# A convolution block split between ScalarE and GpSimd, in a one-core decoder-layer kernel on Trainium2

## The chip, the cores and the metric

The kernel runs on one core of one Trainium2 chip. A core has a matrix engine (TensorE, PE in the profile), three engines that work on whole tiles (VectorE or DVE, ScalarE or ACT, GpSimd or POOL), a queue engine for transfers (SyncE or SP), an on-chip memory of 128 partitions (SBUF) and an accumulator memory (PSUM). Each engine runs its own instructions in the order in which they were written into the program, and waits on semaphores for the others.

The metric is the device time of one execution in microseconds (us). The median of three runs before the change is 1310.73 us.

## The reference

One layer of a decoder over 1,024 tokens of 1,024 channels: RMS norm, one input projection, a token mixer whose two halves work side by side (an RWKV-7 head group of 8 heads and a causal convolution of 512 channels and 31 taps), an output projection, and a gated feed-forward network with a short convolution of its own. The part that the change touches is the convolution:

```python
c = u[..., :D_CONV] * jax.nn.sigmoid(u[..., D_CONV:])
c = _causal_dwconv(c, cconv_w, cconv_b)        # 31 taps, each channel by itself
c = jax.nn.silu(_layer_norm(c, cln_g, cln_b))  # over the 512 channels
mix = jnp.concatenate([rwkv_out, c], axis=-1) @ w_out
```

Each channel's output is a sum over 31 shifted copies of its input, each times one weight, plus a bias. All is in float32.

## The kernel before, in words

The tokens are worked in two halves of 512 (`h` 0 and 1), each of two quarters (0 to 3). Channels lie on partitions, tokens run along the tile. Matrix products are made exact by splitting both operands into a high and a low part: a weight tile `wr` comes by DMA, ACT casts it to `wh`, and POOL (or a kept copy in memory) supplies the low part `wl` (L158); every product is then three matmuls (`h` by `wh`, the low part of `h` by `wh`, `h` by `wl`). The names `h_314`, `h_315` and so on are these pairs for one block of normed channels, written by ACT (L271, high) and DVE (L273, low).

The convolution has four blocks of 128 channels for each half, `conv(h, i)`. Its input `c` (128 x 542, with the 30 tokens before the half) is made by `glu_in`. `conv` keeps a running sum `acc` in the PSUM bank `pc`, of which there is one. ACT starts it with the first tap and the bias (L407), DVE adds the other thirty taps, one instruction for each (L410), and the last of them writes the result `co` to SBUF. `conv_norm` then transposes the four `co` of a half on PE and normalises them, and `w_out` projects them.

The mixer's recurrence is worked by quarter. A quarter's `inverses` inverts small triangular blocks with a chain of 28 short instructions on DVE, alternately L585 (`sub`, a product) and L587 (`dw`, a sum), with all tensors in SBUF. In front of it stand two transposes (L576), and POOL sets parts of `dw` with memsets (L578, L579). `merge` takes the chain's result: a transpose (L595), two more (L599), and PE's matmuls `pe<-dw,l` in between. Then chunks of 64 tokens run in sequence through `recurrence`, with PE writing `xs`, DVE adding state (`r`, L719), and POOL or ACT scaling states (`XG`, L700, L698). PE's projection of the second half is interleaved with this.

The order of the work is set by a scheduler: each part is written in a stream that has a priority number, and the scheduler places instructions on each engine by priority and by its own estimate of times, so that a change in one block moves others.

```python
PRIO = {"first": -1000, "top": 100000, "rwkv": 1000, "norm": 200000, "conv": 300000, "proj": 400000}
BUFS = {..., "co": 4, "po": 1, "c": 4, "t2": 2}
```

The smaller number comes first. In addition `conv(0, 2, W[1].mark)` and `conv(0, 3, W[1].mark)` are held until the last transpose (L599) of quarter 1's `merge` has been issued. The tag `t2` (two buffers of 128 x 512 in SBUF) is used for the normalised rows in `conv_norm` and for one copy in `glu_in`.

Of the kernel before, what the change touches and what calls it, by code (L numbers as in the profile page):

```python
# [15 lines left out]
AF = mybir.ActivationFunctionType  # L16
ALU = mybir.AluOpType
# [4 lines left out]
P = 128  # L22
# [3 lines left out]
HALF = 512  # L26
# [9 lines left out]
CONV_W = 31  # L36
# [58 lines left out]
class Trunk:  # L95
# [281 lines left out]
    def glu_in(self, h, hs, st, i):  # L377
# [19 lines left out]
            nc.gpsimd.tensor_copy(self.ccarry[:, i], c[:, HALF:])  # L397
        st["c", i] = c


    def conv(self, st, i):

        nc = self.nc
        c, co, acc = st["c", i], self.tl("co", [P, HALF]), self.bank("pc")
        st["co", i] = co
        w = lambda j: self.par("cw", i * CONV_W + j)
        nc.scalar.activation(acc, c[:, :HALF], AF.Identity, scale=w(0), bias=self.par("cb", i))  # L407
        for j in range(1, CONV_W):
            out = co if j == CONV_W - 1 else acc
            nc.vector.scalar_tensor_tensor(out, c[:, j:j + HALF], w(j), acc, ALU.mult, ALU.add)  # L410
# [671 lines left out]
    def mixer(self, sts):  # L1082
        nc, tc = self.nc, self.tc
        W = [None] * 4
        mixes = [None] * 2

        def project(h, hs, names):
            with self.stream("proj"):
                for n in names.split():
                    if n == "w":  # L1090
                        self.wa_in(h, hs, sts[h])
                    elif n == "g":
                        self.gate_in(h, hs, sts[h])
                    elif n[0] == "u":
                        self.glu_in(h, hs, sts[h], int(n[1]))
                    else:
                        self.rkv_in(h, hs, sts[h], (n[0], int(n[1])))

        def weave(*parts):

            with self.stream("rwkv"):
                parts = list(parts)
                while parts:
                    parts = [p for p in parts if next(p, parts) is None]

        def quarter(q):
            W[q] = SimpleNamespace(off=(q % 2) * QUARTER, st=sts[q // 2], GD=[], bon=[], R=[], CA=[], CK=[])
            return self.elementwise(W[q])
# [43 lines left out]
        def conv(h, i, behind=None):  # L1152

            with ExitStack() as gate, self.stream("conv"):
                if behind is not None:
                    gate.enter_context(tc.issue_after(behind.ins))
                self.conv(sts[h], i)

        def conv_norm(h):
            with self.stream("conv"):  # L1160
                self.conv_norm(sts[h])
# [28 lines left out]
        prepare(0)  # L1190
        project(0, hs, "u0 u1")
        conv(0, 0)
        conv(0, 1, W[0].mark)
        project(0, hs, "u2 u3")
        hs = self.pairs("h")
# [2 lines left out]
        prepare(1)  # L1198
        project(1, hs, "k0 k1 w r0 r1")
        weave(quarter(2))  # L1200
        conv(0, 2, W[1].mark)
        conv(0, 3, W[1].mark)
        conv_norm(0)
        project(1, hs, "u0 u1 u2 u3")
        prepare(2)
# [104 lines left out]
```

## Time and profile before

| | before |
|---|---|
| median of 3 runs | 1310.73 us (1307.76 to 1311.3) |
| profiled execution, time | 1310.48 us |
| its span in the profile | 1308.7 us |
| mean granted clock of TensorE | 0.984 |
| PE busy | 1260.4 us |
| DVE busy | 864.0 us |
| ACT busy | 678.4 us |
| POOL busy | 462.6 us |

The span runs from the first to the last instruction; the time of the execution is 1.8 us longer. Busy time of an engine is no bound by itself: what counts in a stage is which engine the others wait for there. A row of a group reads: line, engine, operation, result and operands with their shapes, count, busy time and mean length of one in ns, then the engine's idle time in front of them and who ended it. A row of the timeline reads: start, length, engine, line, operation, operands, count, and in square brackets the idle time in front with its releaser. In a table by stage each engine's busy time stands with the number of its instructions.

In the profiled execution `conv(0, 2)` runs on DVE from 243 to 271 us and `conv(0, 3)` from 273 to 306 us; its input `c` is there at 188 us.

### The profile page before, as it was taken

How to read it: one execution, taken by the hardware profiler on the slowest of the kernel's cores; microseconds unless marked ns; L12 is line 12 of the kernel's file. 1: busy time of each engine (PE TensorE's matmuls, PEld its weight loads, DVE VectorE, ACT ScalarE, POOL GpSimd, SP SyncE). 2: the span in 40 equal slices, each digit the busy share in tenths (PEclk: the TensorE clock that was granted, in tenths of full speed). 3: DMA queues.
4: the chain of work that ended last, by engine and by line, in shares of the span. 5: the costliest groups of instructions: out<-in, count | busy, mean ns of one | idle time of the engine just before them, and what ended most of it. 6: DMA issues, size and time to landing. Idle time of an engine off the chain costs nothing.

```text
span 1308.7 us, 22940 instructions
## 1 busy us (share of the span) xinstructions
PE 1260.4 (96%) x8580; PEld 1018.6 (78%) x8580; DVE 864.0 (66%) x1520; ACT 678.4 (52%) x1354; POOL 462.6 (35%) x412
## 2 busy tenths in 40 slices
PE   5999989999999989999999999999999999999996
PEld 4767767777779867878799788888888888888884
DVE  5276997996789989995521364355455438479567
ACT  6563663656855765657642464443433445444451
POOL 4343320111123322444462466676766540000001
PEclk9999989999999989999999999999999999999998
DMA  6554332243333351222354765666564433335326
GB/s 236 160 146 125 115 112 90 83 145 113 115 110 106 119 181 43 73 66 78 100 161 126 265 211 167 194 183 195 173 207 137 120 92 113 94 110 164 105 65 209
DMA packets 97167, 176.77 MB, mean 135 GB/s; under 512 B 10560, under 2 KB 17088, under 8 KB 97056
## 3 DMA queue, kind: packets, MB, share of 16 engines
q1 hardware_dynamic: 97056, 175.31, 43.5%
q8 instruction: 67, 1.10, 0.4%
q14 instruction: 44, 0.36, 0.1%
HBM read 139.62 MB, written 35.65 MB: 134 GB/s over the span
## 4 chain that ended last, share of the span: by engine, by line
PE 77%; DVE 14%; ACT 4%; DMA 2%; issue 2%; POOL 1%; SPq 0%; POOLq 0%; ACTq 0%; DVEq 0%
PE pb L131 63%; PE pe L131 5%; DVE pc L410 4%; PE pn L131 3%; PE xs L131 3%; DVE dw L587 1%; PE pe L146 1%; DMA x<-x1d 1%; DVE pt L479 1%; DVE nrow L971 1%; DMA pt<-mixd 1%; DVE kk L480 1%; POOL wl L158 1%; PE pc L146 0%; DVE m L158 0%
## 5 line engine op out<-in xcount | busy, mean ns | idle before, releaser
L131 PE MATMUL pb<-f,wh 128*128 128x512 f32 x1408 | 444.5, 396 | 3.6 <-ACT pb L782 1.8
L158 POOL TENSOR_TENSOR wl<-wr,wh 128x512 fp32r<-128x512 f32 (+1 forms) x240 | 316.3, 1319 | 360.9 <-ACT wh L158 332.4
L158 ACT CAST wh<-wr 128x512 fp32r<-128x512 f32 (+1 forms) x279 | 171.5, 615 | 296.0 <-PE pb L131 142.3
L131 PEld LDWEIGHTS pb<-f,wh 128*128 128x128 f32 x1408 | 265.1, 189 | 63.9 <-ACT pb L782 2.0
L131 PE MATMUL pb<-f,wl 128*128 128x512 f32 x704 | 280.6, 399 | 1.7 <-POOL wl L158 1.5
L131 PE MATMUL pb<-h,wh 128*128 128x512 f32 (+3 forms) x720 | 230.0, 399 | 1.9 <-ACT wh L158 1.0
L888 DVE SCALAR_TENSOR_TENSOR acc<-pb,params,acc 128x511 f32<-128x511 f32 (+1 forms) x128 | 95.4, 745 | 184.8 <-ACT acc L883 124.0
L410 DVE SCALAR_TENSOR_TENSOR pc<-c,params,pc 128x512 f32<-128x512 f32 x232 | 174.1, 751 | 8.3 <-ACT pc L407 4.4
L131 PEld LDWEIGHTS pb<-f,wl 128*128 128x128 f32 x704 | 133.1, 189 | 34.6 <-POOL wl L158 3.9
L131 PEld LDWEIGHTS pb<-h,wh 128*128 128x128 f32 (+2 forms) x720 | 132.0, 189 | 34.4 <-ACT wh L158 2.7
L131 PE MATMUL pb<-h,wl 128*128 128x512 f32 (+3 forms) x360 | 146.3, 406 | 2.7 <-POOL wl L158 2.5
L153 POOL TENSOR_TENSOR ss<-var,mhalf 128x1 f32<-128x1 f32 x16 | 11.0, 693 | 229.7 <-DVE ss L952 203.3
L131 PE MATMUL pb<-w,a 128*128 128x512 f32 x366 | 89.8, 393 | 0.0
L131 PEld LDWEIGHTS pb<-h,wl 128*128 128x128 f32 (+2 forms) x360 | 67.8, 188 | 21.8 <-POOL wl L158 5.1
L131 PE MATMUL pb<-wh,a 128*128 128x512 f32 x240 | 81.5, 396 | 0.0
L131 PEld LDWEIGHTS pb<-w,a 128*128 128x128 f32 x366 | 68.7, 188 | 16.1
L928 POOL TENSOR_TENSOR b<-b,b 128x512 f32<-128x512 f32 x44 | 57.0, 1295 | 0.9
L888 DVE SCALAR_TENSOR_TENSOR pt<-pb,params,pt 128x511 f32<-128x511 f32 (+1 forms) x48 | 35.7, 744 | 31.5 <-ACT ecarry L885 31.0
L131 PEld LDWEIGHTS pb<-wh,a 128*128 128x128 f32 x240 | 45.1, 188 | 10.6
L700 POOL TENSOR_TENSOR XG<-r,GE 64x256 f32<-64x256 f32 x30 | 20.8, 696 | 85.5 <-DVE r L719 80.8
L883 ACT ACTIVATE acc<-pb,params 128x512 f32<-128x512 f32 x64 | 49.5, 773 | 1.8 <-PE pb L131 1.8
L131 PE MATMUL pb<-wl,a 128*128 128x512 f32 x120 | 47.7, 397 | 0.0
(301 smaller groups left out, 2038.8 us busy)
## 6 DMA issues: line engine op xcount, KB each, us to landing
wr<-ffn_up SPq DMA_DIRECT2D x176, 256.0 KB, 2.7
wr<-w_in SPq DMA_DIRECT2D x80, 256.0 KB, 2.9
b<-ffn_down SPq DMA_DIRECT2D x44, 256.0 KB, 3.9
sums<-b SPq DMA_DIRECT2D x44, 256.0 KB, 2.4
wr<-sums SPq DMA_DIRECT2D x44, 256.0 KB, 2.7
lows<-wl SPq DMA_DIRECT2D x40, 256.0 KB, 3.2
wl<-lows SPq DMA_DIRECT2D x40, 256.0 KB, 2.6
wr<-ffn_down SPq DMA_DIRECT2D x33, 256.0 KB, 2.7
```

The costliest lines, as they stand in the source:

```text
L131: return self.nc.tensor.matmul(out, lhsT, rhs, start=start, stop=stop, skip_group_check=skip)
L146: self.nc.tensor.transpose(out, in_, self.con("ident")[:n, :n])
L158: return self.nc.scalar.copy(hi, src), eng.tensor_tensor(lo, src, hi.bitcast(F32), ALU.subtract)
L410: nc.vector.scalar_tensor_tensor(out, c[:, j:j + HALF], w(j), acc, ALU.mult, ALU.add)
L479: nc.vector.tensor_tensor_scan(sg[:, l], self.con("scan"), sg[:, l], 0.0, ALU.mult, ALU.add)
L480: nc.vector.scalar_tensor_tensor(kk[:, l], k[:, l], self.par("k_k", 2 * pp + l), kk[:, l], ALU.mult, ALU.mult)
L587: nc.vector.tensor_tensor(dv[:, j + 1:, :j], dv[:, j + 1:, :j], tv, ALU.add)
L700: nc.gpsimd.tensor_tensor(x[64:128], R[64:128, gs], w.GE[64:128, c, gs].unsqueeze(2).broadcast_to([64, 4, CH]), ALU.mult)
L883: nc.scalar.activation(acc, ps, AF.Identity, scale=w(2), bias=self.par("fb", ch))
L888: nc.vector.scalar_tensor_tensor(acc[:, o:], ps[:, :HALF - o], w(j), acc[:, o:], ALU.mult, ALU.add)
L928: sub = lambda o, x, y, op=ALU.subtract: nc.gpsimd.tensor_tensor(o, x, y, op)
L971: nc.vector.tensor_tensor(out, a, b, op)
```

## The change

One block, `conv(0, 3)`, is computed by a new function. ACT writes the first tap with the bias into `co` in SBUF, then multiplies each of the other thirty taps into a tile `ct` (tag `t2`), and POOL adds each tile to `co`. PSUM and DVE have no part in it. The call stands ahead of that for `conv(0, 2)` and is not held by `W[1].mark`. `conv(0, 2)` and all other blocks stay as they were.

```diff
+    def conv_pool(self, st, i):
+
+        nc = self.nc
+        c, co = st["c", i], self.tl("co", [P, HALF])
+        st["co", i] = co
+        w = lambda j: self.par("cw", i * CONV_W + j)
+        nc.scalar.activation(co, c[:, :HALF], AF.Identity, scale=w(0), bias=self.par("cb", i))
+        for j in range(1, CONV_W):
+            ct = self.tl("t2", [P, HALF])
+            nc.scalar.activation(ct, c[:, j:j + HALF], AF.Copy, scale=w(j))
+            nc.gpsimd.tensor_tensor(co, co, ct, ALU.add)
...
-                self.conv(sts[h], i)
+                (self.conv_pool if (h, i) == (0, 3) else self.conv)(sts[h], i)
...
+        conv(0, 3)
         conv(0, 2, W[1].mark)
-        conv(0, 3, W[1].mark)
         conv_norm(0)
```

The new lines shift those below them by 12: what is L578 in the kernel before is L590 after. Its own lines are L407 (first tap), L410 (taps) and L411 (adds).

The scheduler places the new instructions among those of other streams, at three places that matter here. The first is ACT where the second half's channels are handed to PE. `c_305` is the block's input, `h_314` and `h_316` the first two channel pairs. Before:

```order
L698 COPY XG_356_2135<-xs0_95 64x256
L698 COPY XG_357_2138<-xs1_96 64x256
L641 COPY l8_207_1125<-pe_247_1486 32x8x32
L271 ACTIVATE h_314_1928<-pe_330_1944,params_72 128x512
L271 ACTIVATE h_316_1930<-pb_331_1951,params_72 128x512
```

After:

```order
L710 COPY XG_356_2135<-xs0_95 64x256
L710 COPY XG_357_2138<-xs1_96 64x256
L653 COPY l8_207_1125<-pe_247_1486 32x8x32
L410 ACTIVATE t2_492_3150<-c_305_1882,params_72 128x512
L410 ACTIVATE t2_493_3153<-c_305_1882,params_72 128x512
L271 ACTIVATE h_314_1928<-pe_330_1944,params_72 128x512
L271 ACTIVATE h_316_1930<-pb_331_1951,params_72 128x512
```

Two taps now stand ahead of the first copy of the channels; on DVE, four L410 of `conv(0, 1)` (L422 after) stand ahead of the first L273, where two stood.

The second place is POOL around quarter 1's inverse chain, from the memsets of `dw` at its start to the memset of `l8_366` behind its end (L604 before, L616 after). `co_491` is the block's sum, `t2_...` the taps, `wl_439` and `wl_442` are low parts of weights. Before:

```order
L158 TENSOR_TENSOR wl_439_2857<-wr_437_2854,wh_438_2856 128x256
L578 MEMSET dw_98 128x16x16
L579 MEMSET dw_98 128x16
L158 TENSOR_TENSOR wl_442_2875<-wr_440_2872,wh_441_2874 128x256
L700 TENSOR_TENSOR XG_394_2592<-r_383_2272,GE_130_729 64x256
L604 MEMSET l8_366_2208 32x32x32
```

After:

```order
L590 MEMSET dw_98 128x16x16
L411 TENSOR_TENSOR co_491_3148<-co_491_3148,t2_507_3195 128x512
L591 MEMSET dw_98 128x16
L411 TENSOR_TENSOR co_491_3148<-co_491_3148,t2_508_3198 128x512
L411 TENSOR_TENSOR co_491_3148<-co_491_3148,t2_509_3201 128x512
L158 TENSOR_TENSOR wl_439_2857<-wr_437_2854,wh_438_2856 128x256
L411 TENSOR_TENSOR co_491_3148<-co_491_3148,t2_510_3204 128x512
L712 TENSOR_TENSOR XG_394_2592<-r_383_2272,GE_130_729 64x256
L411 TENSOR_TENSOR co_491_3148<-co_491_3148,t2_511_3207 128x512
L411 TENSOR_TENSOR co_491_3148<-co_491_3148,t2_512_3210 128x512
L158 TENSOR_TENSOR wl_442_2875<-wr_440_2872,wh_441_2874 128x256
L616 MEMSET l8_366_2208 32x32x32
```

Six adds now stand between the memsets, fifteen stand before them and nine behind.

The third place is PE where it takes the chain's result (`pe_386<-dw_98`). `pb_436` and `pb_444` are projection sums. Before:

```order
L131 MATMUL pb_436_2853<-h_328_1942,wl_442_2875 64x512
L146 MATMUL xs1_96<-const_73,v_163_906 64x128 x2
L131 MATMUL pb_444_2895<-h_314_1928,wh_446_2898 128x512
L131 MATMUL pb_444_2895<-h_315_1929,wh_446_2898 128x512
L131 MATMUL pe_386_2329<-dw_98,l8_342_2059 32x16 x64
```

After:

```order
L131 MATMUL pb_436_2853<-h_320_1934,wl_439_2857 64x512
L131 MATMUL pb_436_2853<-h_322_1936,wh_441_2874 64x512
L131 MATMUL pb_436_2853<-h_323_1937,wh_441_2874 64x512
L131 MATMUL pe_386_2329<-dw_98,l8_342_2059 32x16 x64
L131 MATMUL xs0_95<-r_383_2272,l8_186_1034 64x64
```

Before, all 24 matmuls of `pb_436` and two of `pb_444` stand ahead of it; after, 14 of `pb_436`. The other ten and the two of `pb_444` follow.

On DVE the L410 of `conv(0, 3)` are gone; the first statistics of half 0's normalisation follow two instructions behind the last tap of `conv(0, 2)`.

## The prediction

> **What bounds the kernel now.** I read the page's busy times first, then a table of busy time by stage, then the two lines that carry the convolution, and only then single instructions around it.
>
> ```profile
> PE 1260.4 (96%) x8580; PEld 1018.6 (78%) x8580; DVE 864.0 (66%) x1520; ACT 678.4 (52%) x1354; POOL 462.6 (35%) x412
> PE 77%; DVE 14%; ACT 4%; DMA 2%; issue 2%; POOL 1%; SPq 0%; POOLq 0%; ACTq 0%; DVEq 0%
> L410 DVE SCALAR_TENSOR_TENSOR pc<-c,params,pc 128x512 f32<-128x512 f32 x232 | 174.1, 751 | 8.3 <-ACT pc L407 4.4
> ```
>
> TensorE (PE) is busy 96% of the span and carries 77% of the chain that ended last; VectorE (DVE) carries 14%. The convolution's multiply-adds (L410) are the largest DVE group, 751 ns each. By stage (columns: stretch and its length, then PE, PEld, DVE, ACT, POOL busy, PE clock, DMA share, GB/s):
>
> ```profile
> 185.00:200.00 15.00, 12.63 (x59) 9.38 (x58) 14.89 (x24) 8.19 (x16) 0.21 (x1) 0.57 0.08 23
> 200.00:330.00 130.00, 129.84 (x1377) 101.34 (x1376) 107.86 (x202) 77.04 (x153) 15.83 (x25) 1.00 0.36 111
> 330.00:367.00 37.00, 36.01 (x262) 27.93 (x261) 23.77 (x51) 27.02 (x57) 5.25 (x6) 1.00 0.37 115
> 367.00:420.00 53.00, 50.07 (x445) 43.27 (x444) 52.64 (x100) 25.95 (x54) 18.55 (x16) 0.99 0.35 105
> 420.00:450.00 30.00, 29.23 (x439) 27.36 (x439) 27.37 (x44) 24.11 (x54) 10.23 (x10) 0.96 0.40 126
> 450.00:480.00 30.00, 26.64 (x379) 20.65 (x375) 24.23 (x50) 18.18 (x50) 9.56 (x11) 0.89 0.57 180
> 480.00:500.00 20.00, 16.89 (x174) 13.24 (x173) 19.30 (x49) 16.66 (x41) 3.61 (x6) 1.00 0.19 67
> ```
>
> From 200 to 330 us, where the moved work stands before and after, PE idles 0.16 us in 130. DVE's relief there is worth nothing by itself, while any new wait of PE costs its full length. What DVE's relief can win lies later: PE idles 0.99 + 2.93 + 0.77 + 3.36 + 3.11 = 11.2 us from 330 to 500, and DVE is full (52.64 of 53) only from 367 to 420, where 2.93 of these lie.
>
> **What moves, and what one piece costs.**
>
> ```profile
> L482 ACT ACTIVATE pt<-pt 128x512 f32<-128x512 f32 x8 | 5.0, 631 | 9.9 <-DVE pt L479 9.9
> L928 POOL TENSOR_TENSOR b<-b,b 128x512 f32<-128x512 f32 x44 | 57.0, 1295 | 0.9
> 213.08 1.19 POOL L700 TENSOR_TENSOR XG<-r,GE 64x256 f32<-64x256 f32 x2 [24.79 <-DVE r L719]
> ```
>
> Gone are 30 L410 on DVE (30 x 0.75 = 22.5 us). New are 31 activations on ScalarE (ACT), nearest row 631 ns, so 31 x 0.63 = 19.5 us less the one initialisation that was there, and 30 adds on GpSimd (POOL), nearest row 1,295 ns, so 38.9 us. In the order of the changed program they stand between about 187 us (channels there) and 257 us (end of the adds). POOL has the room: it was idle 24.79 us before 213.08 alone. ACT has less: 77 busy of 130, and about 19 more in the first 60 of them, so about nine tenths full there.
>
> **Term 1, the taps ahead of the norm's copies: +1.3.** At 187.8 us ACT and DVE hand the channels of the second half to PE, which already waits:
>
> ```profile
> 187.81 0.69 ACT L271 ACTIVATE h<-pe,params 128x512 fp32r<-128x512 f32 x1
> 187.87 1.54 DVE L410 SCALAR_TENSOR_TENSOR pc<-c,params,pc 128x512 f32<-128x512 f32 x2
> 189.31 0.75 DVE L273 SCALAR_TENSOR_TENSOR h<-pe,params,h 128x512 fp32r<-128x512 f32 x1
> 190.11 0.69 PE L146 MATMUL pe<-const,mixr 128*128 128x128 f32 x2 [0.93 <-DVE h L273]
> ```
>
> The new order puts two taps ahead of the first L271 on ACT (2 x 0.63), and four L410 instead of two ahead of the first L273 on DVE (1.54 us more). Both delays run side by side, so 1.3; from 0, if the copies of both engines have slack that I don't see, to 2.
>
> **Term 2, ACT and POOL queues from 195 to 260 us: +2.** Each tap from the third on waits on ACT for the add two before it, because the tag `t2` has two buffers; an ACT that waits holds the weight casts (L158, L174), the evacuations (L338) and the state copies (L688, L721) behind it. PE has no slack here, so every late cast is a PE wait. I walked the rows of both engines through with the durations above and found four waits of 0.4 to 1.5 us, part of them overlapping. Bounds 0 and 5: nothing when POOL keeps ahead, 5 when an add takes 1.4 and the lag is never made up.
>
> **Term 3, the add and the inverse chain block each other: +6.4.** The rows that decide are an earlier stage of the same program, in which POOL runs single weight subtractions (SBUF operands, 128x512) beside DVE's inverse chain (L585 and L587, two small SBUF operands):
>
> ```profile
> 118.54 0.19 DVE L585 TENSOR_TENSOR sub<-dw 128x26 f32<-128x26 f32 x1
> 118.76 1.20 DVE L587 TENSOR_TENSOR dw<-dw,sub 128x26 f32<-128x26 f32 x1
> 119.99 0.20 DVE L585 TENSOR_TENSOR sub<-dw 128x36 f32<-128x36 f32 x1
> 122.48 1.33 DVE L587 TENSOR_TENSOR dw<-dw,sub 128x54 f32<-128x54 f32 x1
> 118.61 1.30 POOL L158 TENSOR_TENSOR wl<-wr,wh 128x512 fp32r<-128x512 f32 x1
> 122.46 1.29 POOL L158 TENSOR_TENSOR wl<-wr,wh 128x512 fp32r<-128x512 f32 x1 [2.54 <-ACT wh L158]
> 157.25 1.70 DVE L497 SCALAR_TENSOR_TENSOR kk<-pt,kk 128x512 f32<-128x512 f32 x1
> 157.11 1.29 POOL L158 TENSOR_TENSOR wl<-wr,wh 128x512 fp32r<-128x512 f32 x1 [2.03 <-ACT wh L158]
> ```
>
> An L587 of 0.2 us takes 1.20 and 1.33 us when it meets a POOL instruction, and ends where that one ends (118.76 + 1.20 = 119.96 against 119.91). L497 next to one takes 1.70. So a DVE instruction with both tensors in SBUF stands still until POOL's is done. L410, whose accumulator lies in PSUM, does not:
>
> ```profile
> L410 DVE SCALAR_TENSOR_TENSOR pc<-c,params,pc x232: 723/754/757, 135.0 to 581.0; 128x512 f32<-128x512 f32 x116
> 401.74 0.74 DVE L410 SCALAR_TENSOR_TENSOR pc<-c,params,pc 128x512 f32<-128x512 f32 x1
> 401.59 1.38 POOL L158 TENSOR_TENSOR wl<-wr,wh 128x512 fp32r<-128x512 f32 x1 [1.71 <-ACT wh L158]
> ```
>
> Its longest of 232 is 757 ns (minimum, median and maximum stand in the row), and one that starts 0.15 us behind a subtraction on POOL still takes 0.74. [...]
>
> The second inverse chain of the first half stands in the middle of the adds:
>
> ```profile
> 229.28 0.18 DVE L585 TENSOR_TENSOR sub<-dw 128x14 f32<-128x14 f32 x1
> 234.35 0.74 DVE L344 SCALAR_TENSOR_TENSOR row<-pb,params,row 128x511 f32<-128x511 f32 x1
> 236.46 0.54 DVE L587 TENSOR_TENSOR dw<-dw,sub 128x44 f32<-128x44 f32 x1
> 239.61 1.14 DVE L595 STREAM_TRANSPOSE dw<-dw 64x512 f32<-64x512 f32 x1
> 243.77 2.20 PE L131 MATMUL pe<-dw,l 32*32 32x16 f32 x128
> 247.31 0.40 PE L131 MATMUL pb<-h,wl 128*128 128x512 f32 x1
> 248.00 0.39 PE L131 MATMUL pb<-h,wl 128*128 128x512 f32 x1
> ```
>
> In the new order six adds stand on POOL between the chain's two ends, with the two weight subtractions for `wl_439` and `wl_442` (half as wide) drawn in between them. Six adds at 1.05 and two halves at 0.6 give 7.5; some fall beside instructions of DVE that read PSUM (0.74 for L344, twice 0.4 for L719) and cost nothing, so 6. The 128x1024 product before the chain (L543, twice, SBUF only) meets adds too: 1.3. Against it stands slack: PE takes the chain's result at 243.77, 3.0 us after it is there (239.61 + 1.14); but the new order has twelve projection matmuls fewer ahead of that row, at three per 0.69 us 2.8 us; and L565 (0.7) now stands behind the chain. So 0.9 of slack. 6 + 1.3 - 0.9 = 6.4, and all of it is PE's, which runs in order: the recurrence and the projection behind that row wait. Bounds: 0, if POOL is so early or late that no adds meet the chain; and 13.8, if POOL is late by four adds more (10 x 1.05 + 1.2 + 2 x 1.05). More can't be, since a later tap waits on ACT behind L615, which waits for the chain's end.
>
> **Term 4, the clock: +1.** In the row from 185 to 200, where PE waits 2.4 us of 15, the clock was granted at 0.57; after a wait of 6 us PE may run slow for some us. 0 to 2.
>
> **Term 5, DVE's relief: -3.** Without the 30 L410 between 273 and 306 us, half 0's normalisation and the second half's convolutions come earlier on DVE, and the full stretch from 367 is thinned. That returns the 2.93 us of PE idle there. The other 8 have other makers by the same view: waits of PE for the row norm and its channels, of which the largest are
>
> ```profile
> PE pb L131 <- DVE f L273: 1.8, 3, 0.9
> PE pe L131 <- ACT dw L659: 1.6, 1, 1.6
> PE xs L146 <- DVE t L776: 1.1, 1, 1.1
> ```
>
> These are latencies in a chain that stays. Bounds 0 and -11. SP's queue gets no new transfer; the order of its weight loads follows PE's, and I cost that at nothing, covered by three raw weight buffers. Two more activation tables could have come with the new activations; the program of the change holds two table loads fewer, so no cost.
>
> **Sum.** 1.3 + 2 + 6.4 + 1 - 3 = +7.7 on the profiled execution's 1310.48 us (span 1308.7, 1.8 around it), which is 0.25 below the median of the runs, 1310.73. That gives 1318.2, say 1318.
>
> **Rivals.**
> *DVE's relief wins (faster).* [...] It decides from where the give-back exceeds the sum of terms 1 to 4 (10.7 by my sum): for it speaks that DVE is at 99% from 367 to 420; against it that PE idles only 11.2 us in all after 330.
> [...]
> [...] POOL lags, ten adds meet the chain: 1.3 + 5 + 13.8 + 2 - 3 = +19, 1330. For it: ACT nearly full, so taps come late; against: POOL's start is early.
>
> **How the numbers follow.** The forecast, +4 to +13: 0.48. The full lock: 0.12. Covered: 0.22. Relief wins: 0.18. About 0.3% (4 us) is what a measurement of this kernel can tell from no change. So slower 0.60, same 0.22, faster 0.18. The range from 1304 to 1331 leaves out about half of the relief's case (0.08) and the end of the full lock (0.06); the forecast alone would be 1314 to 1324.
>
> **What would show it.** Term 3: L585 and L587 of that chain in steps of 1.2 to 1.3 us beside adds, the chain from its first L585 to L595 lasting 16 us or more instead of 11.5, and PE waiting several us for DVE `dw` (L595's line) with a low clock behind it. Terms 1 and 2: PE waits for L273 of 2 us at 190, and for casts (L158, L174) of up to 1.5 between 220 and 245. Term 5: DVE's busy time from 367 to 420 well under 52.6. Adds at 1.3 us. I would be wrong if the chain isn't stretched, if POOL's adds end before 229 us, or if PE's idle from 330 to 500 falls under 3 us.

## The result and the profile after

| | before | after |
|---|---|---|
| median | 1310.81 us (4 runs) | 1329.62 us (4 runs, 1327.62 to 1331.08) |
| ratio to before, 95% interval | | 1.0147 [1.0124, 1.0170] |
| profiled execution: time, span | 1310.48, 1308.7 us | 1331.08, 1329.3 us |
| mean granted clock | 0.984 | 0.977 |

The change costs 18.8 us. It was forecast at +7.7, so the sign was right and the size was not; 1329.6 lies inside the range, at the far end. The page's busy line and the stages, with the columns of the prediction's table:

```profile
PE 1268.7 (95%) x8580; PEld 1025.9 (77%) x8580; DVE 852.3 (64%) x1490; ACT 695.0 (52%) x1382; POOL 497.5 (37%) x442
185.00:200.00 15.00, 11.25 (x60) 7.79 (x61) 14.89 (x24) 9.71 (x18) 0.21 (x1) 0.54 0.10 32
200.00:330.00 130.00, 124.18 (x1283) 95.53 (x1281) 94.26 (x175) 90.36 (x175) 56.09 (x55) 0.96 0.31 94
330.00:367.00 37.00, 35.38 (x296) 27.76 (x295) 34.37 (x61) 26.02 (x56) 3.67 (x5) 1.00 0.40 122
367.00:420.00 53.00, 50.99 (x528) 42.13 (x527) 47.17 (x95) 30.61 (x50) 12.13 (x14) 1.00 0.32 94
450.00:480.00 30.00, 30.00 (x364) 26.09 (x361) 15.04 (x31) 14.50 (x39) 8.84 (x10) 1.00 0.37 104
480.00:500.00 20.00, 13.73 (x197) 10.04 (x196) 18.03 (x52) 14.55 (x36) 5.72 (x9) 1.00 0.48 159
500.00:600.00 100.00, 95.60 (x1054) 79.02 (x1055) 89.43 (x153) 57.63 (x128) 33.84 (x30) 0.88 0.21 63
```

PE now idles 5.8 us from 200 to 330, where the forecast put its waits. But it also idles 6.3 us from 480 to 500 (3.1 before) and 4.4 from 500 to 600, and there the clock was granted at 0.88, where it had been 1.00. A loss shows in two forms, then: PE waits, or it is busy at a lower clock. To add them I use one measure below: the length of a stage less its PE busy time multiplied by the granted clock.

| lost PE time, us | 185 to 330 | 330 to 540 |
|---|---|---|
| before | 8.6 | 16.2 |
| after | 20.1 | 25.5 |

(From rows for 185 to 210, 210 to 270, 270 to 330, 330 to 430 and 430 to 540 us; those that matter most are these, of before and then of after. Their columns behind the length are PE busy, clock, DMA share, GB/s.)

```profile
430.00:540.00 110.00, 102.90 (x1314) 0.97 0.37 114
```

```profile
210.00:270.00 60.00, 55.38 (x660) 0.94 0.28 84
430.00:540.00 110.00, 98.99 (x1376) 0.89 0.35 109
```

So 11.5 us more were lost early and 9.3 late, 20.8 together, against 20.6 between the two profiled executions; from 430 to 540 alone the loss is 21.9 us against 10.2.

**The early loss.** Rows of DVE, POOL, ACT and PE around the second inverse chain:

```profile
228.27 0.72 ACT L410 ACTIVATE t<-c,params 128x512 f32<-128x512 f32 x1 [1.77 <-POOL co L411]
229.02 1.04 ACT L585 COPY l<-l 32x1024 f32<-32x1024 f32 x1
230.09 2.26 DVE L588 STREAM_TRANSPOSE dw<-l 64x512 f32<-64x512 f32 x2 [2.98 <-ACT l L585]
232.38 0.42 DVE L597 TENSOR_TENSOR sub<-dw 128x14 f32<-128x14 f32 x1
233.06 1.26 DVE L597 TENSOR_TENSOR sub<-dw 128x26 f32<-128x26 f32 x1
234.57 1.16 DVE L597 TENSOR_TENSOR sub<-dw 128x36 f32<-128x36 f32 x1
236.72 1.34 DVE L599 TENSOR_TENSOR dw<-dw,sub 128x50 f32<-128x50 f32 x1
240.76 0.75 DVE L344 SCALAR_TENSOR_TENSOR row<-pb,params,row 128x511 f32<-128x511 f32 x1
245.43 1.11 DVE L607 STREAM_TRANSPOSE dw<-dw 64x512 f32<-64x512 f32 x1
232.97 1.30 POOL L411 TENSOR_TENSOR co<-co,t 128x512 f32<-128x512 f32 x1
234.35 1.32 POOL L411 TENSOR_TENSOR co<-co,t 128x512 f32<-128x512 f32 x1
236.69 1.29 POOL L411 TENSOR_TENSOR co<-co,t 128x512 f32<-128x512 f32 x1 [1.02 <-ACT t L410]
241.60 0.51 ACT L469 ACTIVATE kk<-row,params 128x256 f32<-128x256 f32 x1 [4.14 <-DVE row L344]
242.01 1.05 ACT L562 COPY ck<-pe 128x512 f32<-128x512 f32 x2
242.63 2.07 PE L131 MATMUL pe<-pt,const 128*128 128x512 f32 x2 [4.62 <-ACT ck L562]
```

Steps of 0.2 us last 1.2 to 1.3 and end with POOL's adds (four such steps, and two more of 0.42 and 0.65 us). PE's wait of 4.62 us is not at the chain's end but in front of it: L344 stands in DVE's queue in the middle of the chain and came late; ACT stood 4.14 us at L469, which needs L344; the copies L562 behind L469 freed PE's bank late. One blocked queue held a second, and that one a third. L344 came 6.4 us later than before (240.76 against 234.35), and the blocked steps are only about half of that: the chain also began 3.1 us later (232.38 against 229.28). DVE had waited 2.98 us for the copy L585 on ACT, which stood behind a tap that waited 1.77 us for an add.

**The late loss.** The first half's output projection (`pb<-wh,m`) and the first feed-forward matmuls (`pb<-f,wh`), before and then after; the last two numbers are the starts of the first and the last:

```profile
L131 PE MATMUL pb<-wh,m x192: 277/283/629, 389.4 to 456.4; 128*128 128x256 f32 x192
L131 PE MATMUL pb<-f,wh x128: 387/389/504, 499.8 to 558.9; 128*128 128x512 f32 x128
```

```profile
L131 PE MATMUL pb<-wh,m x192: 274/283/680, 400.2 to 481.6; 128*128 128x256 f32 x192
L131 PE MATMUL pb<-f,wh x59: 388/390/502, 528.7 to 559.8; 128*128 128x512 f32 x59
```

The projection ends 25 us later, though only about 9 us more had been lost by then (11.5 early, less 2.4 won back from 330 to 430): the new order puts more of PE's other work ahead of it, 4,079 matmuls up to that point against 3,864. Between its end and the first feed-forward matmul runs a chain of transfers and norms, 43 us long before and 47 after, in which PE has only short dependent work. The same columns for these two stretches, before and then after:

```profile
456.40:499.80 43.40, 36.93 (x456) 0.92 0.44 143
```

```profile
481.60:528.70 47.10, 36.71 (x624) 0.75 0.29 100
```

PE's busy time multiplied by the clock is 34.0 us in the first and 27.5 in the second: more matmuls, but less work. Five-microsecond stretches of after:

```profile
495.00:500.00 5.00, 1.81 (x36) 1.00 0.45 150
500.00:505.00 5.00, 3.60 (x55) 0.66 0.56 206
505.00:510.00 5.00, 2.87 (x103) 0.71 0.21 70
510.00:515.00 5.00, 4.41 (x141) 0.50 0.29 110
515.00:520.00 5.00, 5.00 (x58) 0.50 0.01 3
520.00:525.00 5.00, 5.00 (x50) 0.50 0.01 2
525.00:530.00 5.00, 5.00 (x62) 0.74 0.01 3
```

PE idles for nearly half of the time from 495 to 510, and then works at half clock until about 527.

### The profile page after: what moved, and what is told of

It is laid out like the page before. It is cut to its first block, busy times and chain, and to the rows that moved or that the text cites. A ratio compares the mean times of both kernels' runs of the same rounds, so it can differ in the third digit from the quotient of the medians.

```text
span 1329.3 us, 22991 instructions
## 1 busy us (share of the span) xinstructions
PE 1268.7 (95%) x8580; PEld 1025.9 (77%) x8580; DVE 852.3 (64%) x1490; ACT 695.0 (52%) x1382; POOL 497.5 (37%) x442
## 5 line engine op out<-in xcount | busy, mean ns | idle before, releaser
L422 DVE SCALAR_TENSOR_TENSOR pc<-c,params,pc 128x512 f32<-128x512 f32 x203 | 152.5, 751 | 4.9 <-ACT pc L419 1.2
```

## The experiments

Theory A: the late loss is made by the scheduler's new order on PE, not by the block's work. Rivals: B, it is the early delay passed on; C, it comes with DVE's relief in any order. For the early loss: the blocked pair, against taps in ACT's queue.

### The block left out, and three ways to move work

e1 leaves out the taps and adds (`co` then holds the first tap only):

```diff
-        for j in range(1, CONV_W):
-            ct = self.tl("t2", [P, HALF])
-            nc.scalar.activation(ct, c[:, j:j + HALF], AF.Copy, scale=w(j))
-            nc.gpsimd.tensor_tensor(co, co, ct, ALU.add)
```

> The block's thirty taps and adds are left out (only the first tap with the bias is written), at the place of the changed program: DVE has its relief, ACT and POOL have no new work, nothing can block the inverse chain. The order on PE late in the layer's first part is like that of the changed kernel: the first output projection ends late, with little other work of PE behind it. Theory A (the late loss of 8 us from 330 to 640 us comes from this order, which the scheduler makes when DVE is free of the block): the early loss is gone, the late one stays: PE's idle time plus its clock loss from 330 to 640 is 25 us or more against 19.6 before, and the time about 1316. Theory B (the late loss is the early delay passed on): both are gone, and DVE's relief shows: 1302 to 1308.

Measured: 1327.2 us, ratio 1.0122 [1.0091, 1.0152]. This is the surprise of the study. With neither taps nor adds, and 30 instructions less on DVE, the kernel is nearly as slow as with them.

```profile
210.00:270.00 60.00, 60.00 (x747) 1.00 0.35 102
430.00:540.00 110.00, 98.55 (x1302) 0.84 0.31 99
```

From 210 to 270 us nothing is lost, late 27 us (110 - 98.55 x 0.84). B falls: from 185 to 330 only 1.8 us more were lost than before, too little to pass on. A and C stand; the time was 11 us above A's number.

e2 moves the first output projection to the stream of the highest priority:

```diff
-        with self.stream("proj"):
+        with self.stream("first"):
             self.w_out(0, mixes[0], [sts[0]["co", i] for i in range(4)])
```

> The changed kernel with the first half's output projection put in the stream of the highest priority, so that it ends earlier on PE and more of the other work stands between it and the feed-forward network. Theory A (late order): the early loss of about 10 us stays, PE's idle and clock loss from 430 to 540 us falls from 21.6 us towards the 10.3 of before, and the time falls to about 1319. Theory B (the early delay passed on): the time stays at 1327 to 1330.

Measured: 1331.3 us, 1.0158 [1.0131, 1.0186], no gain; A's number is missed by 12 us, and the time lies nearer to B's, which e1 had ruled out. The projection ended at 462 us instead of 482, but the first feed-forward matmul started at 512.7: the norm's first rows then waited for their transfer (`pt<-mixd`, 6.0 us of DVE's waits), and 430 to 540 lost 18.9 us. An earlier projection alone isn't the order of before.

e3 issues the adds behind the memset that follows the chain (`cleared` is that memset, on POOL):

```diff
-        nc.gpsimd.memset(RT[32:64, :, 0:32], 0.0)
+        w.cleared = nc.gpsimd.memset(RT[32:64, :, 0:32], 0.0)
...
-        conv(0, 3)
+        conv(0, 3, W[1].cleared)
```

> The changed kernel with POOL's adds issued behind the memset that follows the second inverse chain, so that no add runs beside the chain. Theory of the blocked pair: L597 and L599 of that chain go back to 0.2 us each, the chain to 11 us, PE's wait of 4.6 us near 240 and the clock loss behind it go. With theory A (late order its own cause) about 8 us come back, 1321 to 1323; with theory B (late loss is the early one passed on) 15 or more, 1311 to 1315. Against the blocked pair: the time stays within 2 us of 1329.6.

Measured: 1334.3 us, 1.0178 [1.0142, 1.0214]. The chain's steps are back (median 0.21 and 0.20 us), and the wait of 4.62 us is gone; the time is no better (1334.3 against 1329.6; the two intervals overlap). Each such edit draws a new order, and its own draw hides what is tested: 430 to 540 lost 21.9 us again, and from 210 to 270 us, with the chain free, 5.2 us were still lost, against 7.9 in the changed kernel. No theory's number was met: by the time alone the blocked pair would have fallen; the rows show the blocking, and this run doesn't show what it costs.

e4 calls the block where it was called before:

```diff
-        conv(0, 3)
         conv(0, 2, W[1].mark)
+        conv(0, 3, W[1].mark)
```

> The block on ACT and POOL, but called behind the third block as before the change: its adds then stand behind the second inverse chain, from about 250 us on, and the first output projection keeps its earlier place on PE. Theory A and the blocked pair: neither the early nor the late loss, 1307 to 1313. If ACT's taps and POOL's adds cost by themselves (queues): 1315 or more.

Measured: 1325.8 us, 1.0107 [1.0079, 1.0134]. Theory A's numbers are missed by nearly 13 us at the least, and the time is where the other expectation put it (1315 or more, if taps and adds cost by themselves). But the first add starts only at 270 us: with the chain undisturbed and no add beside it, 4.9 us were lost from 210 to 270, and 430 to 540 lost 22.5. Here too the order drawn hides the work.

### The order held fixed

The next runs take the draw out. The order of all instructions of the kernel before, engine by engine and for the DMA queue, is stored, and each instruction is given an order-only edge to the one ahead of it; the block's own instructions are left out of this and stay free.

```diff
+def pin(tc, nc):
...
+        ins = [i for i in nc.cur_bb.bb.instructions if str(i.engine) == "EngineType." + eng
+               and type(i).__name__ != "BassTilePoolBoundary" and i.name not in free]
+        for p, q in zip(order, order[1:]):
+            tc.add_manual_dep(
+                ins[q], ins[p].name,
+                mybir.DependencyInfo(mybir.DependencyClass.NoSync, mybir.DependencyReason.DATA), reason="pin")
...
         Trunk(ctx, tc, a).run()
+        pin(tc, nc)
```

e5 is e1 with this:

> The block's thirty taps and adds are left out, as in the first experiment, but the instructions of all engines and of the DMA queue are pinned to the order in which they stand in the kernel before (without the thirty). Theory A (the late loss comes from the scheduler's new order, not from the relief): idle plus clock loss of PE from 430 to 540 us is that of before, about 10 us, and the time 1304 to 1312. Theory C (DVE's relief by itself bunches the later work, whatever the order): the time stays near the 1327 of the first experiment.

Measured: 1310.4 us, ratio 1.0000 [0.9989, 1.0010].

```profile
430.00:540.00 110.00, 102.38 (x1312) 0.97 0.35 114
```

C falls, A stands. It also gives the price of DVE's relief when nothing else moves: nothing, within 1.4 us.

e6 is the changed kernel with this:

> The changed kernel with everything but the block pinned to the order of the kernel before; the block's taps and adds are left to the scheduler, which puts seven adds beside the second inverse chain. Theory A: the early loss of 8 to 10 us stays (L597 and L599 stretched, a PE wait near 240), the late one goes: 1316 to 1322. Theory C: 1327 to 1332.

Measured: 1321.8 us, 1.0088 [1.0073, 1.0103], 11.2 us above before.

```profile
210.00:270.00 60.00, 52.95 (x631) 0.89 0.24 76
430.00:540.00 110.00, 100.97 (x1466) 0.98 0.36 115
```

The early loss stays (12.9 us in 60), the late one is gone (11.0). Ten of the chain's 28 steps lasted 0.55 to 1.32 us, one of them (0.55) as in the kernel before. PE's largest wait from 184 to 340 us is for L731, which stands in DVE's queue among these steps:

```profile
PE xs L146 <- DVE r L731: 4.6, 2, 3.5
```

e7 is e4 with this:

> The block on ACT and POOL called behind the third block, everything else pinned to the order of before: all thirty adds stand behind the second inverse chain. Theory of the blocked pair with theory A: 5 us or more faster than the pinned changed kernel, 1308 to 1314, L597 and L599 of that chain at 0.2 us. If ACT's taps cost as much by their place in ACT's queue as the blocking does: within 3 us of the pinned changed kernel. Theory C: 1325 or more.

Measured: 1326.7 us, 1.0121 [1.0094, 1.0148], far above what the blocked pair or the taps were to give, and in the range of theory C (1325 or more). But 430 to 540 lost only 11.4 us, so it isn't C's loss. One wait explains it, in the view of PE's waits from 184 to 340 us (total, times, longest):

```profile
PE pc L146 <- POOL co L411: 15.4, 1, 15.4
```

The chain was undisturbed and PE lost nothing from 210 to 270 us. But started that late, POOL's thirty adds end 15 us after the point at which PE, in the order of before, transposes `co` for the norm. In time this run shows a wait for the adds, not the absence of blocking.

e8 changes the order alone, with all work on DVE as before:

```diff
+        conv(0, 3)
         conv(0, 2, W[1].mark)
-        conv(0, 3, W[1].mark)
```

> The kernel before with the fourth block on DVE as it was, only called ahead of the third and not held by the mark; no work is moved to another engine. The scheduler's order changes: the first output projection ends some 70 rows later on PE. Theory A (a changed order alone costs late): 1316 to 1325, with 15 us or more of idle and clock loss from 430 to 540 us. Theory C: 1309 to 1314.

Measured: 1328.9 us, 1.0141 [1.0126, 1.0156].

```profile
430.00:540.00 110.00, 99.56 (x1259) 0.89 0.35 110
```

Not one instruction is added or removed, only the call and its hold are moved, and the time, 4 us above theory A's range, is that of the changed kernel. The loss from 430 to 540 is 21.4 us, as there. That the times agree is chance: this run lost no more than before from 185 to 330 us (8.6), and 34.0 from 330 to 540, where the changed kernel lost 25.5.

### The parts of the early loss, and whose order it is

e9 is e6 with the adds parted around the chain (`cleared` as in e3):

```diff
-            nc.gpsimd.tensor_tensor(co, co, ct, ALU.add)
+            with self.tc.issue_after(cleared.ins) if j > 10 else ExitStack():
+                nc.gpsimd.tensor_tensor(co, co, ct, ALU.add)
```

> As the pinned changed kernel (1321.8 us), but the adds from the eleventh on are issued behind the memset that follows the second inverse chain: ten adds stand ahead of the chain, twenty behind, none beside it. Theory of the blocked pair: the chain goes back to 0.2 us a step, PE's idle and clock loss from 210 to 270 us falls from 12 us to under 3, and the time to 1309 to 1314. If the cost came from the taps in ACT's queue: 1318 or more.

Measured: 1316.9 us, 1.0054 [1.0035, 1.0072].

```profile
210.00:270.00 60.00, 57.25 (x710) 0.94 0.28 85
L598 DVE TENSOR_TENSOR sub<-dw x14: 174/205/636, 230.1 to 239.8; 128x14 f32<-128x14 f32 x2, 128x26 f32<-128x26 f32 x2, 128x36 f32<-128x36 f32 x2, 128x44 f32<-128x44 f32 x2
```

The time lies between the two expectations. The chain is back at a median of 0.2 us a step, and 4 to 5 us came back, with the same taps and adds: 1321.8 - 1316.9 is 4.9, and 4.3 when each is taken from before in its own round (11.2 and 6.9). The intervals of e6 and e9 don't overlap, by a hair. The taps moved too, since each waits for the add two before it: POOL ran no add from 230.0 to 245.7 us, so no tap ran on ACT from about 231.5 to 247. What parts the two causes are the waits: that for L731 (4.6 us in e6) is gone, those for copies on ACT are not. The loss from 210 to 270 is 6.2 us, not under 3: the theory of the blocked pair has its sign and half of the early loss. The rest are waits for copies on ACT (`l` L644 1.8 us, `r` L689 0.9) and the clock behind them.

e10 leaves the adds out and keeps the taps, which then hold `co` to the first tap:

```diff
-            nc.gpsimd.tensor_tensor(co, co, ct, ALU.add)
```

> The thirty adds are left out, the thirty taps on ACT stay; everything else is pinned to the order of before. Theory of the blocked pair: ACT has room and its taps wait for nothing, 1309 to 1313. If ACT's taps hold up casts and copies by themselves: 1316 or more.

Measured: 1314.6 us, 1.0043 [1.0030, 1.0057], between the two expectations. Here the taps have no adds to wait for, and PE waited 5.8 us in all for the channel copies (`h` L273, 184 to 340 us; 1.6 before); it lost 12.8 us from 185 to 210 (25 - 18.45 x 0.66; 8.5 before) and nothing from 210 to 270. So taps in ACT's queue do cost, at that place; how much of it holds in the changed kernel, where the adds space them, this run can't tell.

e11 is e1 pinned in the same manner to the order of the changed kernel:

> The block's thirty taps and adds are left out, and all else is pinned to the order of the changed kernel. Theory A says that the changed kernel's late loss is that order's: idle plus clock loss from 430 to 540 us stays at 18 us or more and the time is 1318 to 1324, the rest up to 1329.6 being the early loss. If the late loss is mostly the early delay passed on, the time is 1308 to 1313.

Measured: 1323.4 us, 1.0099 [1.0072, 1.0126].

```profile
430.00:540.00 110.00, 99.75 (x1329) 0.88 0.33 103
```

In the changed kernel's order, without its taps and adds, 13.5 us of the 18.8 are there, and the late loss (22.2 us) whole. From 185 to 330 us 12.5 us were lost, so the order costs 3.9 us early as well. The work of the block adds 5 to 6 us in this order (18.8 - 13.5, or 1329.6 - 1323.4), 11.2 in that of before; the two parts don't simply add.

e12 is e1 with PE alone pinned to the order of before:

> The block's thirty taps and adds are left out and only PE's instructions are pinned to the order of before; DVE, ACT, POOL and the DMA queue are ordered by the scheduler. If the order on PE is what costs: 1308 to 1313. If the order on the other engines costs as much: 1318 or more.

Measured: 1310.3 us, 1.0007 [0.9992, 1.0021]. To hold PE's order is enough. Whether the order on the other engines would cost by itself stays open: in this run's trace they follow PE's, and by line and tile only a handful of DVE's and POOL's instructions stand elsewhere than in the kernel before.

## Why the prediction was right in sign and wrong in size

- **Terms 1 to 4** came to 10.7 us. In the kernel whose order was held (e6) they measured 11.2, and in the changed kernel 11.5 us more were lost from 185 to 330 than before. That the sums agree is partly luck. PE's idle time there grew by 7.0 us, where terms 1 to 3 had 9.7, and the loss by the lower clock grew by 4.4, where term 4 had 1. And 3.9 of the 11.5 come with the order alone (e11), 7.6 with the block's work. Term 1: PE waited 2.4 us for L273 near 190 instead of 0.9, so +1.4 of 1.3 forecast. Term 2: a wait of its kind held the chain's start back by most of 3.1 us. Term 3 (6.4 with the chain's slack): taking the adds from beside the chain gave 4 to 5 us back (e6 to e9); the four blocked steps took 0.96 to 1.13 us longer than the same steps of before, where I had taken 1.05 for an add. The chain lasted 14.2 us (232.38 to the end of L607), not the 16 or more that I had named as a sign. The share of 1.3 us for L543 didn't come: the two lasted 1.34 and 1.22 us after (as L555), 1.22 and 1.21 before. The wait also came elsewhere, by way of L344, L469 and L562, not at the row I named. Taps took 0.72 us, not 0.63; adds 1.29 in the median, as taken.
- **Term 5 is the step that failed.** I gave DVE's relief -3, with bounds of 0 and -11. DVE's busy time from 367 to 420 fell as foreseen (47.2 of 53), PE's idle time there fell by 0.9 us only, and with the order held the whole relief is worth 0.0 (e5). What came instead has the other sign, and my sum had no term for it: the scheduler put other work ahead of the first output projection, and the norm behind it had less of PE's work to run beside (27.5 us at full clock instead of 34.0). That is +9.3 us from 330 to 540 in the profile, and 13.5 us by e11 for the order as a whole. It isn't the relief's doing alone: the moved call draws such an order with all work left on DVE (e8), and the moved work draws one with the call at its old place (e4). I had read the changed order at three places around 190 to 245 us, and none where the projection ends.
- **Term 4** took the clock as a matter of the early wait alone, and too small: its bounds were 0 and 2, and the early loss by the clock grew by 4.4 us, in e6 by 5.8. Late, where I had given it nothing, it grew by a further 5.9.
- **The rivals.** The relief's case needed a gain that the kernel doesn't have. The full lock, a rival with ten adds beside the chain, named 1330, near the measured time, but the cause was another: the chain was stretched by six steps, not by ten adds, and the rest came from the order. No run shows a lock; what the rows show is DVE steps of 0.2 us that took 1.16 to 1.34 and ended within 0.1 us of an add on POOL.

## What to carry to other kernels

Where a scheduler orders the instructions, an edit's own cost and the new order it draws are two things, and the second can be the larger: leave the edited work out and pin the old order, before believing that a time belongs to the work; left out alone, it drew a third order here (e1). Idle time of one engine is worth nothing until a wait that ends on it is found; thirty instructions off a busy VectorE bought nothing here (e5, ratio 1.0000). And here adds on GpSimd did not fit beside a short VectorE chain in SBUF: an add of 1.29 us turned a step of 0.2 us into one of 1.2 to 1.3, and through in-order queues it held the next engines too (ACT for 4.14 us, PE for 4.62).

## What the runs showed of the hardware that I had not expected

The clock halved without one long wait. From 480 to 530 us of the changed kernel PE's longest single wait was 2.1 us,

```profile
PE pb L131 <- DVE sf L873: 2.1, 1, 2.1
```

and amid several waits of 0.6 to 2.1 us the granted clock went to 0.50. In rows of one microsecond it is 0.50 from about 500 to 503.5, 1.00 again up to 507, and 0.50 from there to about 527.5, through stretches in which PE was busy for 5.00 of 5 us. Around the first fall, from 496.0 to 500.8, PE worked for 0.8 of 4.8 us, between waits of 1.51, 1.36 and 1.15 us; the second falls inside the wait of 2.1. The second time the clock came back only after some 12 us in which PE, with small matmuls (128x128 and smaller), was never idle (515 to 527, busy 12.00 of 12 us at 0.50). What makes the granted clock fall and come back, these runs don't show. What also stays open is which of the moved PE rows matter: e2 shows that an earlier projection is not enough.
